# An encoder block on one core: first rows' transposes moved ahead of q's loads, a Fourier copy ahead of a gate's split, more steps between maxima and splits, and steps between first output loads

## Chip, cores and metric

The kernel runs on one core of one Trainium2 chip. The metric is the device time of one execution in microseconds (us), the median of three runs. All work is in one launch; weights, inputs and outputs lie in HBM.

## The reference, cut to what matters

Two batches of 2048 tokens with 1024 channels share one set of weights and go through the same block:

```
u  = rmsnorm(h) ; z = u @ w_in                      # 1024 -> 2304 columns
q, k, v, ga, f, gf = split(z)                       # 512, 128, 128, 512, 512, 512
q, k = rope(rmsnorm(q)), rope(rmsnorm(k))           # per head, 64 wide
a  = softmax(q k^T / 8) v * silu(ga)                # 8 query heads, 2 key/value heads
fo = (real 2-D DFT of f over positions and 64 channels) @ w_fmix * silu(gf)
h  = h + concat(a, fo) @ w_out
h  = h + (p @ w_ple) * sigmoid(rmsnorm(h) @ w_ple_gate)
y  = rmsnorm(h)
```

Everything is float32 in HBM.

## The kernel before

**Products.** A float32 operand is split into two fp16 halves: a power of two scales it, ScalarE (ACT) writes the high half, and VectorE (DVE) writes what is left as the low half (a "split"). Each product is three fp16 matmuls on TensorE (PE). The scale of a weight needs its largest magnitude: eight maxima on DVE, one for each 128 rows, then a maximum over the partitions on GpSimd (`partition_all_reduce`), then a few small DVE operations (`pow2_all`), and then the eight splits.

**Stages.** `project` (the head of the kernel) takes 16 chunks of 256 rows, eight for each batch. For each chunk it forms q, k and v (`mm_tile`), normalises and rotates them, and runs a "sweep" (`sweep_f`, `sweep_ga`) that forms the Fourier input f (two row tiles), the Fourier gate gf (two row tiles, each followed by a small DFT matmul `first` on the f tile) and the attention gate ga (four parts). A sweep is 66 steps; a step of f or gf is three matmuls of 512 columns, a step of ga three of 256. ACT copies f out of PSUM as `ft` at the start of sweep step 9 (first tile) and step 17 (second tile); gf is taken out at steps 25 and 34, ga at 43, 51, 59 and at the first step of what follows. After the head comes the attention, with "fill" work between its steps: first the second half of the DFT (`fourier2`), then the output projection and the rest (`outp`), which goes on when attention is over.

**Order.** In the head the order of each engine's instructions is the order in which Python issues them: every engine is a queue in which an instruction that waits holds all behind it. SyncE (SP) issues most loads, all transposes (DMA) and most stores, in the same order. Background work (`bg`: the other weights' maxima and splits, then the rows of p in `embed_rows`, then `channel_map`) is a generator. `sweep_part(us)` runs sweep steps until their nominal cost is used up, and after every fifth step (`NBF = 5`) takes one piece of `bg`, a piece ending at a `yield`:

```python
us -= next(sweeps[0])
if done:
    done.append(True)
    if len(done) % NBF == 0:
        next(bg, None)
```

`done` is empty for the first `sweep_part` and has one entry from just before the second. `weight_far` has two load pieces, one piece for each of its eight (or two) maxima, one for the scale, and one for each split with its store; it holds two loads ahead. It is called for wo0, pg0, wp0, wo1, pg1, wp1 (`w_out`, `w_ple_gate`, `w_ple` by column half). Tiles of this work and of the sweep share ten slots, `w2k`.

PSUM has eight banks. `bank()` hands them out by a counter: where it is 0 to 4 modulo 8 the tile is `ps_x` (five banks), else `ps_f` (three).

In the start of `project` the order is: first rows of x, weights of k and v, second rows of x, weights of q, and only then the arithmetic on the first rows (`sq_u`, `newton`, `hi_u`, three maxima, `lo_u` with its transpose). In the last four passes (`iteration(16)` to `iteration(19)`) no new rows are formed; the norm and rotation of the last chunks (`lo_q`, `rope_q`, `hi_q`) go on beside the last sweep.

In the fill, `self.after(ticket, n)` yields None until n more attention steps than the ticket's have been flushed; `defer` puts an instruction at the next flush, `defer_slow` at a later one. `outp` starts beside `fourier2` after its tenth tile (`half`) and goes as far as `yield "go"`: a maximum over both branches (`mix_max`, with a `partition_all_reduce`), the loads of the first output tile (`first`, the last entry of which is a GpSimd product), its split, and then go.

Of the kernel before, what the change touches and what calls it, by code (L numbers as in the profile page):

```python
# [139 lines left out]
class Build:  # L140
# [188 lines left out]
    def weight_far(self, name, src, cols, g, pool):  # L329

        nc, st = self.nc, self.st
        sl, ahead, nk = {}, AH, src.shape[0] // 128

        def load(j):
            if j < 2 * nk:
                sl[j] = pool.tile([128, 512], F32, name="w_st", tag="w2k", bufs=self.nw2k)
                nc.sync.dma_start(sl[j][:, :cols], src[j % nk * 128:(j % nk + 1) * 128, :])

        for j in range(ahead):
            load(j)  # L340
            yield
        mx = st.tile([128, 8], F32, name="w_mx")
        for k in range(nk):
            load(k + ahead)
            self.defer(lambda w=sl.pop(k), k=k: nc.vector.tensor_reduce(
                out=mx[:, k:k + 1], in_=w[:, :cols], op=ALU.max, axis=AX.X, apply_absolute_value=True))
            yield
        f = [None] * nk

        def scale():  # L350
            m = mx
            if g is not None:
                m = st.tile([128, 8], F32, name="w_m2")
                nc.vector.tensor_tensor(out=m[:], in0=mx[:], in1=g[:], op=ALU.mult)
            m1 = st.tile([128, 1], F32, name="w_m1")
            nc.vector.tensor_reduce(out=m1[:], in_=m[:, :nk], op=ALU.max, axis=AX.X, apply_absolute_value=True)
            s, self.sc[name] = self.pow2("w_" + name, m1[:], W_EXP)
            f[:] = [s[:]] * nk
            if g is not None:
                gs = st.tile([128, 8], F32, name="w_gs")  # L360
                nc.vector.tensor_scalar(out=gs[:], in0=g[:], scalar1=s[:], scalar2=None, op0=ALU.mult)
                f[:] = [gs[:, k:k + 1] for k in range(nk)]

        self.defer(scale)
        self.wd[name] = nc.dram_tensor("wd_" + name, (128, 2, nk, cols), F16, kind="Internal").ap()
        yield
        for k in range(nk):
            load(k + nk + ahead)
            w = sl.pop(k + nk)
            o = pool.tile([128, 2, 512], F16, name="w_o", tag="w2k", bufs=self.nw2k)  # L370
            nc.scalar.activation(o[:, 0, :cols], w[:, :cols], AF.Copy, scale=f[k])

            def low(k=k, w=w, o=o):
                nc.vector.scalar_tensor_tensor(out=o[:, 1, :cols], in0=w[:, :cols], scalar=f[k], in1=o[:, 0, :cols],
                                               op0=ALU.mult, op1=ALU.subtract)
                nc.sync.dma_start(self.wd[name][:, :, k, :], o[:, :, :cols])

            self.defer(low)
            yield

    def embed_rows(self, pool):

        nc, st = self.nc, self.st
        src = [self.a[n].rearrange("a o (t r) d -> r (a o t) d", t=NT) for n in ("p_prompt", "p_sample")]
        self.ptd = nc.dram_tensor("ptd", (2 * NT, 128, 4, 128), F16, kind="Internal").ap()
        self.pb = self.keep("pb", [128, 2 * NT])
        tl = {}

        def load(i):
            if i < NT:  # L390
                tl[i] = pool.tile([128, 2, 256], F32, name="p_in", tag="w2k", bufs=self.nw2k)
                j = 2 * i % NT
                nc.sync.dma_start(tl[i][:], src[2 * i // NT][:, j:j + 2, :])

        load(0)
        for i in range(NT):
            load(i + 1)
            x, b = tl.pop(i), self.pb[:, 2 * i:2 * i + 2]
            yield
            nc.vector.tensor_reduce(out=b, in_=x[:], op=ALU.max, axis=AX.X, apply_absolute_value=True)  # L400
            nc.vector.tensor_scalar(out=b, in0=b, scalar1=1e-30, scalar2=None, op0=ALU.max)
            nc.vector.tensor_scalar(out=b.bitcast(I32), in0=b.bitcast(I32), scalar1=0x7F800000,
                                    scalar2=None, op0=ALU.bitwise_and)
            f = st.tile([128, 2], F32, name="p_f")
            nc.vector.tensor_scalar(out=f[:].bitcast(I32), in0=b.bitcast(I32), scalar1=-1,
                                    scalar2=(254 + W_EXP) << 23, op0=ALU.mult, op1=ALU.add)
            hl = pool.tile([128, 2, 2, 256], F16, name="p_hl", tag="w2k", bufs=self.nw2k)
            for t in range(2):
                nc.scalar.activation(hl[:, t, 0, :], x[:, t, :], AF.Copy, scale=f[:, t:t + 1])
            yield  # L410
            for t in range(2):
                nc.vector.scalar_tensor_tensor(out=hl[:, t, 1, :], in0=x[:, t, :], scalar=f[:, t:t + 1],
                                               in1=hl[:, t, 0, :], op0=ALU.mult, op1=ALU.subtract)
            pT = pool.tile([128, 2, 4, 128], F16, name="p_T", tag="w2k", bufs=self.nw2k)
            nc.sync.dma_start_transpose(pT[:].rearrange("p t k r -> p (t k) r"), hl[:].rearrange("p t b c -> p (t b c)"))
            yield
            nc.sync.dma_start(self.ptd[2 * i:2 * i + 2].rearrange("t p k r -> p t k r"), pT[:])
            del x, hl, pT
# [125 lines left out]
    def project(self, P, PU, W, early, wkv, wq, wga, bg, mid):  # L544
# [7 lines left out]
        n = len(steps)  # L552
# [177 lines left out]
        def sweep_part(us):  # L730

            while us > 0 and sweeps:
                try:
# [5 lines that stand above are left out]
                        if len(done) % NBF == 2:  # L739
                            next(self.ahead, None)  # L740
                except StopIteration:
                    del sweeps[0]
# [16 lines left out]
        def until(g, word):  # L759
            while next(g) != word:  # L760
                pass

        def iteration(i):
            nonlocal stores, stores_next
            if ok(i + 4):
                load_x(i + 4, 0)
            if ok(i - 1):
                load_rope(i - 1)
            stores, stores_next = stores_next, []
            for f in stores:  # L770
                f()
            del stores[:]
            if ok(i + 3):
                sq_u(i + 3)
            sq = square_z(i - 1) if ok(i - 1) else None
            if ok(i - 1) and i > 2:
                VL.pop((i - 1, 1))()
            if ok(i - 3):
                lo_q(i - 3)
            if ok(i - 2):  # L780
                rope_q(i - 2)
            rs = None
            if ok(i - 1) or ok(i + 2):
                rs = newton(i - 1 if ok(i - 1) else None, i + 2 if ok(i + 2) else None, sq)
            if ok(i):
                mm_tile(i, 0)
            sweep_part(1000.0 if i < n else (5.0, 5.0, 5.0, 100.0)[i - n])
            if ok(i - 1):
                norm_q(i - 1, rs)
            if ok(i + 2):  # L790
                hi_u(i + 2)
                for tt in range(CH):
                    lo_u(i + 2, tt)
            if ok(i + 4):
                load_x(i + 4, 1)
            if ok(i - 2):
                hi_q(i - 2)
            if ok(i):
                VL.pop((i, 0))()
            if ok(i):  # L800
                mm_tile(i, 1)
                append(i)
            if i == n - 3:
                early()
            if i == n + 3:
                self.drain(bg)
                self.drain(self.ahead)
                for f in stores_next:
                    f()
                del stores_next[:]  # L810
# [4 lines left out]
        both(load_x, 0)  # L815
        until(wkv, "loaded")
        both(load_x, 1)
        until(wq, "loaded")
        sq_u(0)
        newton(None, 0, None)  # L820
        hi_u(0)
        for _ in range(3):
            next(wkv)
        both(lo_u, 0)
        until(wkv, "split")
        both(mm_kv, 0)
        until(bg, "loaded")
# [28 lines left out]
        del stores_next[:]  # L856
        append(0)
        until(bg, "split")
        sweep_part(10.0)
        sq_u(2)  # L860
        newton(None, 2, None)
        hi_u(2)
# [3 lines left out]
        until(bg, "split")  # L866
        next(bg)
        done.append(True)
        sweep_part(12.0)
        mid()  # L870
        sq_u(3)
        make_u(3, 0)
# [441 lines left out]
    def outp(self, pool0, ow, open_pool):  # L1314
# [147 lines left out]
        first = load(0)  # L1462
        for f in first[:-1]:
            f()
        yield None
        first[-1]()
        yield from self.after(TM.pop(0))
        yield from self.after(split(0), 2)
        yield "go"
        pool = open_pool()  # L1470
        (wp, gfin), later = self.out_consts(pool)
# [270 lines left out]
```

## Time and profile before

| | before |
|---|---|
| median of three runs | 2787.02 us (2786.7 to 2787.8) |
| the profiled execution | 2787.78 us |
| its span, first to last instruction | 2786.0 us |
| PE busy | 2679.6 us, 96% |
| DVE, POOL, ACT busy | 61%, 59%, 44% |
| granted TensorE clock, mean | 0.987 |

The profiled execution's time is 1.78 us more than its span and 0.76 us more than the median. A row of a timeline has start, duration (both us), engine, line, operation, the tile written and those read, the count of instructions merged into the row, and in brackets how long the engine was idle before it and what ended the wait. SPq and the like are instructions that issue DMAs. A busy share of PE says that a matmul was under way, not how fast it went.

### The profile page before, as it was taken

The page shows a single profiled execution, that of the slowest core. Times are in us where ns is not written, and L with a number is a line of the kernel's source. Part 1 is how long each engine was busy: PE and PEld are TensorE (multiplying, and loading weights), DVE is VectorE, ACT ScalarE, POOL GpSimd, SP SyncE. Part 2 cuts the span into 40 slices and gives each one's busy share as a digit, 9 for nine tenths or more (in the row PEclk, how much of TensorE's full clock was granted, in tenths as well). Part 3 has the DMA queues.
Part 4 walks back from the last instruction along what each step waited for, and adds up shares of the span by engine and source line. Part 5 has one row for each costly group of instructions (what it writes and reads, how often), then busy time and mean ns, then how long its engine had stood idle before and what let it go on. Part 6 is the DMA issues. An engine that isn't in the chain of part 4 may idle for free.

```text
span 2786.0 us, 40443 instructions
## 1 busy us (share of the span) xinstructions
PE 2679.6 (96%) x15332; PEld 1183.4 (42%) x15332; DVE 1691.5 (61%) x2467; ACT 1212.5 (44%) x2047; POOL 1631.6 (59%) x1394
## 2 busy tenths in 40 slices
PE   6799998999998989999999999999999999999998
PEld 3455565565655543333333333333333333333333
DVE  6755546564455765666666666665665665566645
ACT  4433323342224544454544454444444444544442
POOL 1223324242335877777768777767667767677770
PEclk9899999999999999999999999999999999999999
DMA  8467757673427653123221223222322222223223
GB/s 230 142 199 192 200 166 185 174 186 84 139 70 233 216 173 107 46 56 79 64 61 51 61 61 97 78 55 56 74 67 56 61 78 61 54 60 85 56 52 93
DMA packets 418532, 296.37 MB, mean 106 GB/s; under 512 B 259456, under 2 KB 360000, under 8 KB 418336
## 3 DMA queue, kind: packets, MB, share of 16 engines
q1 hardware_dynamic: 405424, 252.01, 34.7%
q0 software_dynamic: 12912, 41.77, 4.5%
q8 instruction: 120, 1.97, 0.3%
q14 instruction: 76, 0.62, 0.1%
HBM read 149.50 MB, written 86.51 MB: 85 GB/s over the span
## 4 chain that ended last, share of the span: by engine, by line
PE 77%; DVE 3%; ACT 1%; issue 1%; POOL 1%; DMA 1%; DVEq 0%; ACTq 0%; POOLq 0%
PE ps_f L429 31%; PE ps_o L1187 15%; PE ps_s L1122 14%; PE ps_x L429 9%; PE ps_m L1149 4%; PE ps_f L1221 1%; PE ps_f L1173 1%; PE ps_f L1041 1%; PE ps_f L995 1%; ACT p L1125 1%; DMA hT<-h_hl 1%; PE ps_x L894 0%; DVE h_hl L1429 0%; DVE a_mx L1157 0%; DVE mh L1352 0%
## 5 line engine op out<-in xcount | busy, mean ns | idle before, releaser
L1130 POOL TENSOR_TENSOR acc<-acc,p 128x1024 f32<-128x1024 f32 x384 | 910.9, 2372 | 245.0 <-ACT p L1125 185.2
L1125 ACT ACTIVATE p<-ps_s,s_scale 128x512 f32<-128x512 f32 x1024 | 648.4, 684 | 748.5 <-PE ps_s L1122 729.3
L1157 DVE TENSOR_REDUCE a_mx<-ps_m 128x1 f32<-128x1024 f32 x499 | 610.3, 1223 | 584.5 <-PE ps_m L1149 583.8
L1187 PE MATMUL ps_o<-p,v 128*64 128x512 f32 x2048 | 465.3, 596 | 0.0
L429 PEld LDWEIGHTS <-uc 128*128 128x128 f16 x3072 | 301.3, 98 | 309.0 <-DMA uc<-hl 23.1
L1122 PE MATMUL ps_s<-q,k 64*128 64x512 f16 x3072 | 425.2, 379 | 6.5 <-ACT p L1125 6.4
L429 PE MATMUL ps_f<-w_pg,hT 128*128 128x512 f16 x1464 | 352.7, 382 | 7.0 <-DMA hT<-h_hl 6.8
L1187 PEld LDWEIGHTS ps_o<-p,v 128*64 128x64 f32 x2048 | 141.6, 137 | 256.5 <-issue 247.5
L1122 PEld LDWEIGHTS <-k 64*128 64x128 f16 x3072 | 115.7, 94 | 307.7 <-issue 236.4
L429 PEld LDWEIGHTS <-hT 128*128 128x128 f16 x1536 | 139.3, 98 | 213.8 <-issue 63.5
L1128 POOL TENSOR_TENSOR acc<-p,p 128x1024 f32<-128x1024 f32 x64 | 150.8, 2357 | 107.8 <-ACT p L1125 107.6
L1149 PE MATMUL ps_m<-k,q 64*128 64x512 f16 x998 | 192.8, 377 | 13.7 <-DVE a_mx L1157 13.7
L429 PE MATMUL ps_f<-w_wo,mh 128*128 128x512 f16 x744 | 181.8, 380 | 4.6 <-DVE mh L1352 4.6
L429 PE MATMUL ps_f<-w_wo,mT 128*128 128x512 f16 x744 | 180.8, 380 | 0.0
L429 PEld LDWEIGHTS <-w_ga 128*128 128x128 f16 x1536 | 153.7, 100 | 37.8 <-issue 17.5
L911 POOL DMA_DIRECT2D gfd<-gt x32 | 19.8, 620 | 228.1 <-DVE gt L939 228.1
L1203 ACT ACTIVATE tb<-ps_o,a_scale 64x256 f32<-64x256 f32 x128 | 60.1, 469 | 162.6 <-PE ps_o L1187 161.8
L929 POOL DMA_DIRECT2D agd<-gat x64 | 35.1, 549 | 147.4 <-DVE gat L939 147.4
L429 PE MATMUL ps_x<-uc,w_ga 128*128 128x256 f16 x1032 | 117.8, 275 | 0.3 <-ACT ge L896 0.3
L1223 DVE RECIPROCAL ps_f<-ps_f 128x256 f32<-128x256 f32 x64 | 112.4, 1756 | 7.2 <-PE ps_f L1221 7.2
L429 PEld LDWEIGHTS <-mh 128*128 128x128 f16 x768 | 68.7, 98 | 108.1 <-issue 33.3
L429 PEld LDWEIGHTS <-mT 128*128 128x128 f16 x768 | 70.0, 98 | 98.9 <-issue 25.4
(283 smaller groups left out, 3330.7 us busy)
## 6 DMA issues: line engine op xcount, KB each, us to landing
q<-qTd SPq DMA_DIRECT2D x256, 64.0 KB, 2.2
ag<-agd SPq DMA_DIRECT2D x64, 256.0 KB, 4.5
out<-h POOLq DMA_DIRECT2D x31, 512.0 KB, 4.0
x<-in_x_prompt SPq DMA_DIRECT2D x16, 512.0 KB, 4.9
w_st<-in_w_out SPq DMA_DIRECT2D x32, 256.0 KB, 4.5
gfd<-gt POOLq DMA_DIRECT2D x32, 256.0 KB, 2.7
gd<-ge POOLq DMA_DIRECT2D x32, 256.0 KB, 3.4
agd<-gat POOLq DMA_DIRECT2D x64, 128.0 KB, 2.7
```

The source lines that it names most:

```text
L429: self.nc.tensor.matmul(ps, lhs(ia, k), rhs(ib, k), start=(i == 0), stop=(i == 3 * ks - 1))
L929: nc.gpsimd.dma_start(self.agd[s][1, r * 128:(r + 1) * 128, c * n:(c + 1) * n], gt[:, :n])
L995: nc.tensor.matmul(o, fT[:, r, y, :], self.bd[:, y, r, :], start=True, stop=x is None)
L1122: nc.tensor.matmul(S[u][e][:], w[sl], q[sl].rearrange("p h q -> p (h q)"), start=j == i == 0, stop=i + 1 == len(todo), skip_group_check=True)
L1125: nc.scalar.activation(p[:, e, :], S[u][e][:], AF.Exp, scale=self.sc["s_scale"][:])
L1128: nc.gpsimd.tensor_tensor(out=ACC[u][:], in0=P[u, 0][:], in1=p[:], op=ALU.add)
L1130: nc.gpsimd.tensor_tensor(out=ACC[u][:], in0=ACC[u][:], in1=p[:], op=ALU.add)
L1149: nc.tensor.matmul(ps[c], Q[u][0][sl, h, :], kt[s, kv, half][sl, :, 0, :], start=True, stop=True)
L1157: nc.vector.reduce_max(MX[u][:, h, half, c:c + 1], x, axis=AX.X)
L1187: nc.tensor.matmul(o[64 * e:64 * e + 64, :], vt[s, kv, c // 8][:, c % 8, :], p[:, e, :], start=(j == 0), stop=(j == 7))
L1203: nc.scalar.activation(tb[64 * e:64 * e + 64], ov[64 - 64 * e:128 - 64 * e, e], AF.Copy, scale=self.sc["a_scale"][64 - 64 * e:128 - 64 * e ...
L1223: nc.vector.reciprocal(r, ps[:, 0:256])
```

## The change

```diff
@@ weight_far
         self.defer(scale)
         self.wd[name] = nc.dram_tensor("wd_" + name, (128, 2, nk, cols), F16, kind="Internal").ap()
-        yield
+        for _ in range(3):
+            yield
         for k in range(nk):
@@ embed_rows
         load(0)
+        yield
+        load(1)
+        yield
         for i in range(NT):
-            load(i + 1)
+            load(i + 2)
             x, b = tl.pop(i), self.pb[:, 2 * i:2 * i + 2]
-            yield
             nc.vector.tensor_reduce(out=b, in_=x[:], op=ALU.max, axis=AX.X, apply_absolute_value=True)
...
             nc.vector.tensor_scalar(out=f[:].bitcast(I32), in0=b.bitcast(I32), scalar1=-1,
                                     scalar2=(254 + W_EXP) << 23, op0=ALU.mult, op1=ALU.add)
+            yield
             hl = pool.tile([128, 2, 2, 256], F16, name="p_hl", tag="w2k", bufs=self.nw2k)
@@ project, iteration
-            sweep_part(1000.0 if i < n else (5.0, 5.0, 5.0, 100.0)[i - n])
+            sweep_part(1000.0 if i < n else (6.0, 9.0, 5.0, 100.0)[i - n])
@@ project, start
         both(load_x, 1)
-        until(wq, "loaded")
         sq_u(0)
         newton(None, 0, None)
         hi_u(0)
         for _ in range(3):
             next(wkv)
         both(lo_u, 0)
+        until(wq, "loaded")
         until(wkv, "split")
@@ project, start
         until(bg, "split")
-        sweep_part(10.0)
+        sweep_part(10.4)
...
         done.append(True)
-        sweep_part(12.0)
+        sweep_part(11.6)
@@ outp
         for f in first[:-1]:
             f()
-        yield None
+        yield from self.after([self.nflush], 3)
         first[-1]()
-        yield from self.after(TM.pop(0))
-        yield from self.after(split(0), 2)
+        yield from self.after(TM.pop(0), 2)
+        yield from self.after(split(0), 1)
         yield "go"
```

`weight_far` has two more empty pieces between the scale and the first split. `embed_rows` loads two tiles ahead instead of one, and the copies that make p's high half go from the maximum's piece into a piece of their own. In the last passes the first two sweep parts get more steps. The two transposes of the first rows are issued ahead of the eight loads of q's weights. The first part of the first sweep goes one step further, and the second as much less. In `outp` some four flushes instead of one fill piece lie between the first loads and the product, two more between product and split, and one less behind the split.

## Rows read from the trace of the kernel before

**Rows 1.** The profile page: span, and busy time of PE and its weight loads, DVE, ACT and GpSimd (POOL) with the share of the span.

```profile
span 2786.0 us, 40443 instructions
...
PE 2679.6 (96%) x15332; PEld 1183.4 (42%) x15332; DVE 1691.5 (61%) x2467; ACT 1212.5 (44%) x2047; POOL 1631.6 (59%) x1394
```

**Rows 2.** The waits of PE in the head (0 to 870 us), the greatest: instruction, what ended the wait, us in total, times, longest.

```profile
PE ps_f L894 <- ACT ft L904: 27.0, 3, 12.5
```

**Rows 3.** Timeline of the start: low halves of the first rows, loads of q's weights, the first rows' transposes, maxima of q's weights, the first matmuls (k and v), the split of q's weights, the matmuls of q.

```profile
10.87 2.48 DVE L627 SCALAR_TENSOR_TENSOR hl<-x,rsq_z,hl 128x1024 f16<-128x1024 f32 x2 [0.24 <-ACT hl L618]
...
11.90 3.52 SPq L292 DMA_DIRECT2D w_t<-in_w_in  x4
...
15.85 7.42 SPq L422 DMA_TRANSPOSE uc<-hl  x2
...
20.50 2.46 DVE L300 TENSOR_REDUCE w_mx<-w_z 128x1 f32<-128x512 f32 x4
...
23.12 8.24 PE L429 MATMUL ps_x<-wr_kv,uc 128*128 128x256 f16 x48 [23.12 <-DMA uc<-hl]
...
31.54 2.73 DVE L323 SCALAR_TENSOR_TENSOR wr_q<-w_z,w_gs,wr_q 128x512 f16<-128x512 f32 x4
32.34 10.41 PE L429 MATMUL ps_x<-wr_q,uc 128*128 128x512 f16 x47 [0.72 <-DVE wr_q L323]
```

**Rows 4.** Timeline of the first sweep: first `ft`, a DFT matmul without a wait, the split of the gate's weight (high halves on ACT, low ones on DVE), and PE behind the second `ft`.

```profile
71.09 0.68 ACT L904 ACTIVATE ft<-ps_x,inv_f 128x512 f32<-128x512 f32 x1
...
73.73 1.02 PE L894 MATMUL ps_x<-ft,dft1x 128*128 128x512 f32 x2
...
86.78 1.33 ACT L322 ACTIVATE w_ga<-w_qn,w_gs 128x512 f16<-128x512 f32 x2 [8.00 <-DVE w_gs L316]
...
88.86 4.05 DVE L323 SCALAR_TENSOR_TENSOR w_ga<-w_t,w_gs,w_ga 128x512 f16<-128x512 f32 x6
...
92.41 2.08 PE L894 MATMUL ps_f<-ft,dft 128*128 128x512 f32 x2 [12.48 <-ACT ft L904]
...
94.28 4.22 PE L429 MATMUL ps_f<-uc,w_ga 128*128 128x256 f16 x24
```

**Rows 5.** Busy time of each engine in two stretches behind a stall; the eighth column is the granted clock of PE.

```profile
92.40:97.20 4.80, 4.79 (x16) 2.76 (x17) 4.66 (x19) 4.23 (x8) 2.35 (x4) 0.50 0.47 158
97.20:105.00 7.80, 7.80 (x74) 6.95 (x73) 7.14 (x39) 1.56 (x4) 1.08 (x2) 1.00 0.20 76
```

**Rows 6.** Timeline of the second sweep, where wo0 gets its scale: last DVE step of the maximum, the maximum over partitions, first splits, `ft`, PE, and the copy `ge` that frees the bank for which the gate's second part waits.

```profile
135.48 0.15 DVE L356 TENSOR_REDUCE w_m<-w_mx 128x1 f32<-128x8 f32 x1
138.90 0.38 POOL L254 PARTITION_ALL_REDUCE p_mm<-w_m  x1 [5.92 <-issue]
...
139.87 1.33 ACT L371 ACTIVATE w_o<-w_st,w_wo_s 128x512 f16<-128x512 f32 x2 [13.84 <-DVE w_wo_s L265]
...
141.83 2.08 PE L894 MATMUL ps_x<-ft,dft 128*128 128x512 f32 x2 [6.10 <-ACT ft L904]
...
146.79 0.59 ACT L896 ACTIVATE ge<-ps_x 128x512 f32<-128x512 f32 x1
...
147.43 2.78 PE L429 MATMUL ps_x<-uc,w_ga 128*128 128x256 f16 x24 [0.31 <-ACT ge L896]
```

**Rows 7.** Timeline of the fifth sweep, where wo1 gets its scale.

```profile
296.15 0.38 POOL L254 PARTITION_ALL_REDUCE p_mm<-w_m  x1 [6.00 <-issue]
...
299.68 5.28 PE L429 MATMUL ps_f<-uc,w_ga 128*128 128x256 f16 x24 [3.92 <-DVE gat L939]
```

**Rows 8.** Timeline of the eighth sweep, where the rows of p begin: the first maximum, PE, and a copy that waits for a slot.

```profile
447.90 0.69 DVE L400 TENSOR_REDUCE pb<-p_in 128x2 f32<-128x512 f32 x1 [3.92 <-DMA p_in<-in_p_prompt]
...
450.76 2.08 PE L894 MATMUL ps_f<-ft,dft 128*128 128x512 f32 x2 [8.68 <-ACT ft L904]
...
452.63 4.24 PE L429 MATMUL ps_f<-uc,w_ga 128*128 128x256 f16 x24
...
457.05 0.60 ACT L896 ACTIVATE ge<-ps_f 128x512 f32<-128x512 f32 x1 [2.27 <-DMA ptd<-p_T]
```

**Rows 9.** Timeline of the end of the head: the last chunk's `hi_q`, PE behind its stall, the first attention matmul, and the first load of the Fourier fill.

```profile
845.58 1.06 ACT L703 ACTIVATE qs<-t 128x1024 f16<-128x1024 f32 x1 [12.99 <-POOL t L691]
...
847.88 2.08 PE L894 MATMUL ps_f<-ft,dft 128*128 128x512 f32 x2 [5.79 <-ACT ft L904]
...
862.29 0.39 PE L1122 MATMUL ps_s<-mr,kone 64*128 64x512 f16 x2 [1.02 <-DVE gat L939]
...
865.71 0.80 SPq L969 DMA_DIRECT2D g_in<-gd  x2
```

**Rows 10.** The same load by its tile (first of the two), from issue to landing, and the first Fourier matmul on PE.

```profile
DMA to landing us min/median/max: 4.2/4.2/4.2
...
870.38 2.82 PE L1041 MATMUL ps_f<-c,g_in 128*128 128x128 f32 x16
```

**Rows 11.** Timeline of the attention about the maximum over both branches: GpSimd's first product behind it, PE, the first output tile's split on ACT, PE.

```profile
990.66 2.33 POOL L1130 TENSOR_TENSOR acc<-acc,p 128x1024 f32<-128x1024 f32 x1 [9.81 <-issue]
...
998.56 0.61 PE L1149 MATMUL ps_m<-k,q 64*128 64x512 f16 x2 [9.80 <-DVE a_mx L1157]
...
1003.86 1.15 ACT L1347 ACTIVATE mh<-ag,mix_s 128x1024 f16<-128x1024 f32 x1 [15.96 <-POOL ag L1333]
...
1006.12 0.37 PE L1122 MATMUL ps_s<-q,k 64*128 64x512 f16 x1 [1.65 <-ACT p L1125]
```

## The prediction

> **What bounds the kernel now.** I read the page, then the waits of PE, then the timeline about each long wait. PE is busy in 96% of the span, the others in 61% or less [rows 1], so what counts is where PE stands still, and how fast it runs behind that. PE's list of waits has six long stalls, and each edit lies beside one. Three, 27.0 us together, wait for `ft` [rows 2]: ACT had to make the copy behind a split whose scale was late. They are 12.48 us in the first sweep [rows 4], 8.68 us at the rows of p [rows 8] and 5.79 us at the end of the head [rows 9]. A fourth `ft`, at wo0, costs 6.10 us [rows 6]; at wo1 PE stands 3.92 us for a bank [rows 7]; at the maximum over both branches 9.80 us [rows 11]. Together 46.8 us.
>
> A stall costs more than its length. Behind the 12.48 us PE had a granted clock of 0.50 (the 1.2 GHz level) for about 5 us, then 1.00 [rows 5]: the two DFT matmuls took 2.08 us instead of 1.02 and 24 gate matmuls 4.22 us [rows 4] instead of 2.78 [rows 6], so 2.5 us more. The stall of 3.92 us costs the same: 5.28 for 2.78 [rows 7].
>
> The question is what comes next in each stage once ACT is out of the way. In the middle of the head PE feeds itself, and a removed stall stays removed; at the start and at the end a chain over the other engines sets the time.
>
> **The transposes ahead of q's loads: +2.5 us.** The low halves of the first rows are done at 13.4 (10.87 + 2.48); the transposes were issued at 15.85 behind q's loads, and k's and v's matmuls began at 23.12. They could now begin at about 18, when their weights' split is under way (an estimate from these rows). But q's matmuls, next on PE, don't wait for that: they began at 32.34 with the low half of q's weights, at the end of a DVE chain that is busy nearly throughout (maxima 20.50, split 31.54) [rows 3]. So k and v end near 26 instead of 31.4, and PE stands still for 5 to 6 us ahead of q. After 3.92 us it lost 2.5 us; I take +2.5. The eight loads are issued from about 17 on; at 0.88 us each [rows 3] and the 4.2 us to landing of a load of that size [rows 10] the first four are there by about 24, where their maxima end at 23.0. A wait there can reach the 7.42 us that the two transposes held SP [rows 3], less some 5 us of lead, so 2.5 us. Bounds: 0 (the clock stays up) to +5. This delay runs on through q and the first sweep, since DVE's maxima for gf and so the gate's split stand behind them. f's eight loads, next on SP, are wanted only after q's split, which covers them.
>
> **The Fourier copy, and wo0's pieces: -2.4 us.** 10.0 was used up after 16 steps of 0.64, 10.4 after 17, and the 17th begins with the copy; 11.6 ends where 12.0 did. So `ft` stands ahead of `sq_u(2)` and costs ACT 0.67 us, by which all behind it, the gate's split too, is late. PE then goes through its DFT matmul at 80 and stops at the gate itself, whose first product needs the split: low halves end at 92.91, now 93.6. That product ended at 98.50 (94.28 + 4.22) [rows 4], so PE has 4.9 us.
>
> They don't last. Two empty pieces move wo0's first split from step 9 of the second sweep to step 20 (bg pieces come after steps 5m + 16 now, 5m + 15 before), so `ft` passes it, and the 6.10 us go. But the scale is asked for at step 5, and DVE's small operations stand right behind it: DVE is done with the maximum at 135.48, GpSimd yields it at 138.90 after 5.92 us in which it waits for nothing shown, and the first split runs at 139.87 [rows 6]. Gate part two needs the bank that `ge` frees, and `ge` stands behind that split. So: 139.87 + 0.67 late + 0.67 split + 0.67 + 0.59 for the two copies = 142.5, where it began at 147.43 [rows 6]. That is 4.9 us for both edits, less 2.5 us for a PE that has again stood about 6 us: -2.4. Bounds: 0, and -12.1 (4.9, 6.10 and 1.06 of slow DFT matmuls) if the chain is no limit.
>
> The 5.92 and 6.00 us recur at each such maximum [rows 6, 7]. The Trainium skill (GPSIMD Engine Reference, Instruction dispatch) says that the first call of a freshly loaded GpSimd kernel pays about 6 us of loading, with no instruction to show for it; the rows agree. Taken alone it says that pieces between scale and split take none of it away, and the sum would be the second rival's.
>
> **wo1: -6.4 us.** The pieces added earlier (2 each at wo0, pg0, wp0, wo1) shift its scale from step 31 of the fifth sweep to step 62. At 31 DVE stood still with gf's second tile and all the gate's still to take out, and three `ps_f` banks were full; at 62 three gate parts are out. 3.92 + 2.5 [rows 7]. Counting banks for the other scales (steps 44, 53, 35, 44 of sweeps 3, 4, 7, 8) I find none where PE would run out within 6 us. Bounds: -6.4 to 0 (another place stalls instead).
>
> **Rows of p: -10.0 us.** The copies stand at step 18 now, behind `ft` at 17, and the loads two tiles ahead, so DVE's 3.92 us for the load go too. 8.68 + 1.06 + 1.46 (4.24 for 2.78) = 11.2 [rows 8]. I give 1.2 back: in this sweep the gate's third part needs a bank that a late DVE frees. Bounds: -11.2 to -6.
>
> **Last passes: 0.** Ten and fifteen steps instead of eight and eight put both `ft` and the first gate copy ahead of the last `hi_q`, and PE is spared 5.79 us and 1.06 of slow DFT matmuls. But the first Fourier matmul, four attention steps on, needs a load that SP issues at 865.71 and that lands 4.2 us later, 869.9 [rows 9, 10]; PE was there at 870.38. SP is held by the last chunk's transposes and stores, these by `hi_q` at 845.58, and that by GpSimd [rows 9]; no edit touches this chain. So PE comes about 7 us early and waits. Bounds: -6.9, and +2.5 (it is slow after the wait).
>
> **`outp`: -1.7 us.** The 9.80 us are DVE's wait for GpSimd, which came back at 990.66, 9.81 us after its maximum; no edit touches that. ACT stood 15.96 us before the split because the product was late, and PE lost 1.65 to that [rows 11]; with six flushes more it doesn't. Bounds: -1.7 to 0; the later go is hidden by the end of `fourier2`.
>
> **Sum.** +2.5 - 2.4 - 6.4 - 10.0 + 0 - 1.7 = -18.0; 2787.8 - 18.0 = 2769.8 for the profiled execution, 0.76 less for the median: 2769.0.
>
> **Rivals.**
> *All stalls go.* If no chain limits, 0 - 12.1 - 6.4 - 11.2 - 6.9 - 1.7 = -38.3, and 2787.0 - 38.3 = 2748.7. For it: each stall's releaser is passed. Against: 139.87 and 869.9 hang on other engines.
> *GpSimd's 6 us move along.* DVE still stands through each, so wo0 and wo1 give nothing: +2.5 - 10.0 - 1.7 = -9.2: 2777.8. Against: of the six such maxima of far weights only wo0's and wo1's stand beside a stall of PE.
> *Slots run out (slower).* Far weights hold two loaded tiles ten steps longer, and the rows of p three tiles instead of two, of ten slots. ACT already waited 2.27 us for one [rows 8]. If each of the sixteen turns adds that on PE's path: 36.3 us, and 2787.0 + 18.3 = 2805. It decides from eight turns on. Against: PE stood for none of them before.
> *No change that can be told* (within 0.2%, 5.6 us, about what a measurement of this kernel can tell): the other engines' chains take all back. Against: at wo1 and at the rows of p, 16.4 us of the sum, the rows show no such chain.
>
> **How the numbers follow.** Forecast 0.60, all go 0.13, GpSimd's move along 0.13, slots 0.07, no change 0.07. Faster 0.86, same 0.07, slower 0.07. Three quarters of the way from the forecast to the first rival is 2754; the second rival and half of the way from it to no change 2782. What lies outside is the slots, no change, and the far part of the first rival, about 0.2.
>
> **What would show it.** Right: matmuls of k and v begin near 18 and q's run slow; no `ft` in PE's waits; PE stands about 7 us at the gate's split and 6 us ahead of gate part two in the second sweep; nothing at wo1; a new wait of about 6 us, of the first Fourier matmul for its load; 9.8 us as before at the maximum, without ACT's 15.96. Wrong: q's maxima wait for loads; ACT or DVE waits for slots reach PE; the end of the head comes 7 us sooner.

## The result and the profile after

The changed kernel took 2769.88 us (median of six runs, 2765.7 to 2777.6), the kernel before 2786.08 us in the same comparison (2782.5 to 2787.8). The ratio is 0.9947, 95% interval 0.9932 to 0.9962: faster. The forecast was 2769.0 us within 2754 to 2782. The total is right; two terms of the sum are not. In the second of the two profiles below their errors cancel, which is luck; in the first only one of them shows. Two executions, one with the transposes undone (2803.55 us, the profiled one) and one with the stores moved (3101.08 us), ran at a mean granted clock of 0.967 and 0.848 where all others had 0.985 or more; they stand outside the medians, and the first one's trace is not used.

The profiled execution took 2765.67 us and is the fastest of its six. So a second profile of the same kernel (the first experiment, 2770.24 us) stands beside it below.

The page of the changed kernel, span and busy time, answers to [rows 1]. PE's busy time fell by 4.7 us and the span by 22.1: what went is standing still.

```profile
span 2763.9 us, 40442 instructions
...
PE 2674.9 (97%) x15332; PEld 1181.3 (43%) x15332; DVE 1684.7 (61%) x2467; ACT 1211.4 (44%) x2047; POOL 1630.8 (59%) x1394
```

PE's waits of the changed kernel up to 1060 us (what ended the wait, us in total, times, longest). Of the waits for `ft` [rows 2] 0.6 us is left. Other names are long instead: the split of q's weights, the split of the gate's, the copy `ge` (0.31 us before [rows 6]), and `g_in`.

```profile
PE ps_m L1153 <- DVE a_mx L1161: 13.7, 5, 9.6
PE ps_f L433 <- ACT w_ga L322: 7.3, 1, 7.3
PE ps_x L433 <- ACT wr_q L322: 7.3, 1, 7.3
PE ps_f L1045 <- DMA g_in<-gd: 5.2, 1, 5.2
PE ps_s L1126 <- ACT p L1129: 4.5, 11, 0.8
PE ps_x L433 <- ACT ge L900: 3.1, 1, 3.1
```

The best view of such a change is the start of the same matmul in both traces. Below, for each place, its start minus the start in the kernel before (negative is earlier); the places are named by their time before. The first line is the sum on record.

```
place (us before)       42.6  106.2  155.3  307.7  464.6    800    873   1200    end
prediction, cumulated   +2.5           0.1   -6.3  -16.3  -16.3  -16.3  -18.0  -18.0
changed kernel         +2.85  -1.81  -4.40 -11.27 -22.58 -20.58 -21.14 -19.89  -22.1
the same, 2nd profile  +3.91  -0.75  -4.63  -6.36 -17.68 -15.25 -16.14 -15.24  -17.6
```

From 307.7 on the second profile lies within 1.4 us of the forecast up to 873. The first is about 5 us earlier from 307.7 on, and that arises at one place, wo1. The rows of the timeline that answer to [rows 3, 6, 9]: start, second sweep, end of the head, each of the changed kernel.

```profile
12.19 5.16 SPq L426 DMA_TRANSPOSE uc<-hl  x2
...
17.40 8.23 PE L433 MATMUL ps_x<-wr_kv,uc 128*128 128x256 f16 x48 [17.40 <-DMA uc<-hl]
...
21.31 2.09 DVE L300 TENSOR_REDUCE w_mx<-w_z 128x1 f32<-128x512 f32 x3 [0.73 <-DMA w_z<-in_w_in]
...
32.94 0.58 PE L433 MATMUL ps_x<-wr_q,uc 128*128 128x512 f16 x1 [7.31 <-ACT wr_q L322]
...
34.03 11.57 PE L433 MATMUL ps_x<-wr_q,uc 128*128 128x512 f16 x47 [0.51 <-DVE wr_q L323]
...
138.56 0.38 POOL L254 PARTITION_ALL_REDUCE p_mm<-w_m  x1 [5.95 <-issue]
...
141.36 4.28 PE L433 MATMUL ps_x<-uc,w_ga 128*128 128x256 f16 x24 [3.13 <-ACT ge L900]
...
833.76 0.39 PE L1126 MATMUL ps_s<-mr,kone 64*128 64x512 f16 x2 [1.08 <-DVE gat L943]
...
843.96 0.80 SPq L973 DMA_DIRECT2D g_in<-gd  x2
...
848.35 3.75 PE L1045 MATMUL ps_f<-c,g_in 128*128 128x128 f32 x16 [5.16 <-DMA g_in<-gd]
```

### The profile page after: what moved, and what is told of

The parts are those of the page before. It is cut to its first block, busy times and chain, and to the rows that moved or that the text cites. A ratio compares the mean times of both kernels' runs of the same rounds, so it can differ in the third digit from the quotient of the medians.

```text
span 2763.9 us, 40442 instructions
## 1 busy us (share of the span) xinstructions
PE 2674.9 (97%) x15332; PEld 1181.3 (43%) x15332; DVE 1684.7 (61%) x2467; ACT 1211.4 (44%) x2047; POOL 1630.8 (59%) x1394
## 4 chain that ended last, share of the span: by engine, by line
PE 78%; DVE 3%; issue 3%; DMA 2%; POOL 1%; ACT 1%; SPq 0%; DVEq 0%; POOLq 0%; ACTq 0%
PE ps_f L433 31%; PE ps_o L1191 15%; PE ps_s L1126 14%; PE ps_x L433 9%; PE ps_m L1153 4%; PE ps_f L1225 1%; PE ps_f L1177 1%; PE ps_f L1045 1%; PE ps_f L999 1%; ACT p L1129 1%; DMA hT<-h_hl 0%; DMA w_st<-in_w_out 0%; DVE a_mx L1161 0%; DMA g_in<-gd 0%; DMA w_st<-in_w_ple_gate 0%
```

## The experiments

Each undoes or adds one thing in the changed kernel, but for two near the end that combine. The ratio is against the kernel before in the same group of runs; the changed kernel's was 0.9947 and 0.9943.

**The changed kernel again.** No edit.

> The changed kernel as it is, beside the undone versions of this group. Its six runs lay between 2765.7 and 2777.6 us, twice the spread of the kernel before. Expected: a median within 2 us of 2769.9. If the spread is of the kernel, some waits differ from one execution to the next, and the profile shows where; if it was chance, the runs lie within 5 us.

Measured: 2770.24 us (2769.6 to 2778.7), ratio 0.9943 (0.9929 to 0.9956). The wide spread is no mark of the change: over 23 runs the kernel before spread as far (2780.8 to 2792.7). But the two profiled executions do differ at one place, wo1, where PE stands in this one, as before [rows 7], and doesn't in the first. Second profile, DVE's first maximum of wo1, its first gate product, and PE:

```profile
286.06 0.69 DVE L345 TENSOR_REDUCE w_mx<-w_st 128x1 f32<-128x512 f32 x1 [4.70 <-DMA w_st<-in_w_out]
...
293.97 0.42 DVE L943 SCALAR_TENSOR_TENSOR gat<-th,ps_f 128x256 f32<-128x256 f32 x1 [3.61 <-DMA gd<-ge]
...
294.44 4.44 PE L433 MATMUL ps_f<-uc,w_ga 128*128 128x256 f16 x24 [3.32 <-DVE gat L943]
```

And the same two on DVE, with PE, in the first profile. DVE is 3 us earlier, early enough for PE, whose row runs through:

```profile
282.88 0.69 DVE L345 TENSOR_REDUCE w_mx<-w_st 128x1 f32<-128x512 f32 x1 [4.68 <-DMA w_st<-in_w_out]
...
290.52 0.42 DVE L943 SCALAR_TENSOR_TENSOR gat<-th,ps_f 128x256 f32<-128x256 f32 x1 [2.62 <-DMA gd<-ge]
...
285.95 8.02 PE L433 MATMUL ps_f<-uc,w_ga 128*128 128x256 f16 x72
```

The wait is not the scale's (that comes at 302.75 and 307.36 now): DVE, which works in order, waits for wo1's first load, and the gate's copies behind it come late. 3.32 us of standing and 1.66 us of slow clock (4.44 for 2.78, with a granted clock of 0.51 from 294.4 to 297.7) are the 5 us.

DVE waits as long for the load in both, 4.70 and 4.68 us, so the 3 us are older. They are there at wo0's fourth split on ACT, in the first profile and in the second:

```profile
146.91 0.72 ACT L372 ACTIVATE w_o<-w_st,w_wo_s 128x512 f16<-128x512 f32 x1 [2.17 <-DMA gd<-ge]
```

```profile
150.28 0.72 ACT L372 ACTIVATE w_o<-w_st,w_wo_s 128x512 f16<-128x512 f32 x1 [4.16 <-DMA gd<-ge]
```

Of these 3.37 us about 1.4 are older still (the first split ran at 139.53 and 140.96), and 1.99 are a longer wait for a slot that a store holds. The background work keeps such a lag. In eight profiles without a piece more at wo1, wo1's first maximum follows the last of wo0's splits by 127.1 to 128.8 us, though these lie between 153.4 and 158.1; in that of the sweep parts at 10.0 it follows by 130.0.

**The transposes behind q's loads again.**

```
+        until(wq, "loaded")
         sq_u(0)
...
         both(lo_u, 0)
-        until(wq, "loaded")
```

> The transposes of the first rows behind q's loads again, all else changed. Theory (absorbed): the 2.85 us that k's and v's second matmuls come later never reach the end, because in the second sweep gate part two waits for the Fourier copy behind wo0's split, whose maximum hangs on SP's loads; PE waits there about 6 us instead of 3.13, and the end moves by -0.5 to +0.5 us. Rival (carried, as the prediction had it): the delay runs on through the head, and the end comes 2.85 us sooner. Either way k's and v's first matmuls begin near 23 instead of 17.4.

Measured: 2766.24 us, ratio 0.9918 (0.9910 to 0.9927), an interval that doesn't touch that of the changed kernel. The rival was right: the move costs, 4.0 us between the medians. I had read "absorbed" from the start of wo0's maximum, which hardly differs before and after; the reason is another one (below, at the second term). Two later kernels with the same undo show the start. In the last one (the output's start, below) q's matmuls run at full clock, 10.41 us, and PE stands 0.72 us:

```profile
23.75 7.60 PE L433 MATMUL ps_x<-wr_kv,uc 128*128 128x256 f16 x48 [23.75 <-DMA uc<-hl]
...
32.57 10.41 PE L433 MATMUL ps_x<-wr_q,uc 128*128 128x512 f16 x47 [0.72 <-DVE wr_q L323]
```

**One empty piece between maximum and split.**

```
-        for _ in range(3):
-            yield
+        yield
```

> One empty piece instead of three between the maximum and the first split of the far weights, all else changed. Theory: gate part two of the second sweep begins near 147 instead of 141.4, which costs 4.4 us up to q's next matmuls, and the stall at wo1 is back, 6.4 to 6.9 us: +9.5 to +11.3 in all, less 1 to 2 us that drift back later. Rival (GpSimd's 6 us move along, whatever stands between): 0. Second rival (wo1 alone): +6.9.

Measured: 2788.95 us, ratio 1.0005 (0.9995 to 1.0015): +18.7, the whole gain, and more than the theory's 11.3. "GpSimd's 6 us move along" falls. PE's long waits of the second and fifth sweep are back, longer than before [rows 6, 7], since PE comes earlier and the scales later; a third, of 3.73 us and for a bank, stands behind the eighth:

```profile
144.34 2.08 PE L897 MATMUL ps_x<-ft,dft 128*128 128x512 f32 x2 [8.59 <-ACT ft L907]
...
304.92 4.29 PE L432 MATMUL ps_f<-uc,w_ga 128*128 128x256 f16 x24 [7.07 <-DVE gat L942]
...
466.84 2.78 PE L432 MATMUL ps_x<-wr_kv,uc 128*128 128x256 f16 x24 [3.73 <-DVE gat L942]
```

By starts it lies 6.7 us behind the second profile at 155.3, 10.3 at 307.7, 10.9 at 464.6, 13.9 at 478, 17.4 at the end, so some 6 us arise outside the two places of the theory. The edit also brings forward all background work behind wo0's scale, the rows of p by twelve pieces; what the pieces do at the scales and what they do as a shift can't be told apart here.

**The last passes at five steps.**

```
-            sweep_part(... (6.0, 9.0, 5.0, 100.0)[i - n])
+            sweep_part(... (5.0, 5.0, 5.0, 100.0)[i - n])
```

> The last passes at five steps each again, all else changed. Theory: the load of the first Fourier matmul sets when PE goes on; PE stands about 6 us for the Fourier copy and no more for the load, and the end moves by 0 to +1 us. Rival (the passes themselves are worth what PE is spared): +7 us.

Measured: 2771.46 us, ratio 0.9935 (0.9922 to 0.9948): no difference. The `ft` stall is back and the load's wait falls from 5.16 to 0.84 us; between 800 and 873 this kernel gains 0.3 us on the kernel before, the changed one 0.6 and 0.9.

```profile
832.45 2.07 PE L898 MATMUL ps_f<-ft,dft 128*128 128x512 f32 x2 [5.80 <-ACT ft L908]
...
855.62 2.02 PE L1045 MATMUL ps_f<-c,g_in 128*128 128x128 f32 x16 [0.84 <-DMA g_in<-gd]
```

**The rows of p as before.**

```
         load(0)
-        yield
-        load(1)
-        yield
         for i in range(NT):
-            load(i + 2)
+            load(i + 1)
...
+            yield
             nc.vector.tensor_reduce(...)
...
-            yield
             hl = pool.tile(...)
```

> The rows of p as before (copies in the piece behind the scale's, loads one tile ahead), all else changed. Theory: PE stands at the first copy again, 8 to 9 us, and runs slow behind it: +10 to +11.3 us, as the aligned starts of the two kernels gave 11.3. Rival (the other pieces have moved the rows of p past the place where it hurts): 0 to +3.

Measured: 2780.32 us, ratio 0.9971 (0.9960 to 0.9983): +10.1 to +10.4 between the medians, +7 to +8 by the ratios. The size is about the predicted one, but not at one place: PE no longer stands 8.68 us [rows 8], but 1.91, 2.88 and 1.68 us at 449, 478 and 643, and 5.2 us are lost between 464.6 and 560. The copies meet the sweeps elsewhere, 12 pieces later.

**The sweep parts at 10.0 and 12.0.**

> The first two sweep parts at 10.0 and 12.0 again, so that the first Fourier copy stands behind the squares and the gate's split, all else changed. Locally PE loses about 6 us in the first sweep (12.5 us of standing for 7.3, and 1.06 us of slow matmuls). Theory (absorbed): 3.13 us of standing and 1.5 us of slow clock in the second sweep go in exchange, and the end moves by +1 to +3. Rival (carried): +6.

Measured: 2769.77 us, ratio 0.9932 (0.9919 to 0.9946): nothing lost. PE stands 12.49 us for `ft` again (95.43), and at 155.3 the kernel is 3.9 us behind the second profile; at 307.7 it is at -6.59, against -6.36, since PE stands only 0.84 us at wo1. Against that profile, what the copy wins is gone again at wo1, where PE goes on when DVE lets it; against the first one, which doesn't stand there, the kernel stays 4.7 us behind. That the copy is worth nothing rests on the medians, not on one profile.

**Five pieces for wo0.**

```
-        for _ in range(3):
+        for _ in range({"wo0": 5, "pg0": 1}.get(name, 3)):
```

> Five empty pieces for wo0 and one for pg0 instead of three each, so that all later pieces stay where they are. The Fourier copy that frees the bank of gate part two then stands ahead of wo0's first split. Theory: the 3.13 us of standing at gate part two and 1.5 us of slow clock go: -4.6 us. Rival: DVE, which still waits for GpSimd until 139, holds the banks or the copies instead, and PE waits for it: 0 to -1.

Measured: 2772.06 us, ratio 0.9946 (0.9933 to 0.9958): nothing. The wait for `ge` is gone and q's next matmuls start at 147.32 instead of 150.65; at wo1 PE then stands 6.53 us instead of 3.32. The theory was right at its place, its sum wrong.

```profile
294.32 5.17 PE L433 MATMUL ps_f<-uc,w_ga 128*128 128x256 f16 x24 [6.53 <-DVE gat L943]
```

**The last stores on GpSimd's queue.**

```
+            dq = nc.gpsimd if i == n - 1 else nc.sync
...
-            nc.sync.dma_start(self.qTd[s][t], qT[:])   (and kTd)
+            dq.dma_start(self.qTd[s][t], qT[:])
```

> The last chunk's stores of q and k go out on GpSimd's queue at the end of the head instead of on SP's, which frees SP about 4.5 us earlier. Theory (SP's chain sets the first Fourier matmul): its load is issued near 839.5 instead of 843.96 and lands near 843.5, PE no longer waits 1.24 us for q nor 5.16 us for the load: -3 to -6 us. Rival: GpSimd stands for the transposes instead, its sums come late and PE waits for their slots: 0 or slower.

The edit also issues them later, behind the head's last background work. Measured: 2768.65 us, ratio 0.9931 (0.9917 to 0.9944): no difference that can be told. PE no longer waits for q. From the first score matmul to the first Fourier matmul it takes 12.73 us (838.69 to 851.42) instead of 14.59, so 1.9 us came of the 4.4 that SP was freed (its q loads start 1.62 us behind the first score matmul, 6.00 us in the changed kernel): the four now take 3.98 us to issue instead of 2.40, and the load 5.13 us to land instead of 4.25. The load is still what PE waits for:

```profile
840.31 3.98 SPq L1114 DMA_DIRECT2D q<-qTd  x4
...
846.25 0.80 SPq L975 DMA_DIRECT2D g_in<-gd  x2
...
851.42 1.86 PE L1047 MATMUL ps_f<-c,g_in 128*128 128x128 f32 x7 [5.42 <-DMA g_in<-gd]
```

**One more piece ahead of wo1's maximum.**

```
+        if name == "wo1":
+            yield
         mx = st.tile([128, 8], F32, name="w_mx")
...
-        for _ in range(3):
+        for _ in range(2 if name == "pg1" else 3):
```

> The changed kernel with one more empty piece between wo1's first loads and its first maximum, and one less at pg1, so that the pieces behind keep their places. In most executions of the changed kernel PE stood about 3 us near 291 for the gate, since DVE had waited 4.7 us for wo1's first load and the tanh and the product behind it then waited for a slot held by a store. Theory (the load comes late for its maximum): DVE no longer waits there, PE doesn't stand and runs at full clock: -4 to -5 us, and a spread like that of the kernel before. Rival (slots: ten are too few whatever the order): DVE's wait goes, the wait for a slot stays, 0 to -1.

Measured: 2768.35 us (2762.4 to 2770.5), ratio 0.9931 (0.9919 to 0.9944). In the profile PE runs through wo1 without a wait (-10.56 at 307.7), though DVE still waits 4.43 us for the load. The medians differ by 1.5 to 1.9 us, within the intervals: not shown. Nor did PE stand about 3 us there "in most executions", as I expected: of the nine profiles with the changed kernel's order at wo1, three have more than 1 us (3.32, 2.03 with the last passes at five steps, 6.53 with five pieces).

**Nine slots.** `self.nw2k = 9`.

> The changed kernel with nine slots of 2 KB instead of ten, nothing else. Theory (the other engines' chain in the second to eighth sweeps is held by slots that stores set free about 4 us after they are issued): waits of ACT and DVE for slots grow, PE stands at wo1 in every execution and at other far weights too: +5 to +20 us. Rival (slots are no limit, the loads and GpSimd are): 0 to +2.

Measured: 2769.79 us, ratio 0.9942 (0.9929 to 0.9956). The rival was right: slots are no limit, and "Slots run out" falls with it, although single rows name a slot's holder (`gd<-ge` above).

**Three together.** The undone transposes, wo1's piece, the stores.

> The changed kernel with three things together: the transposes of the first rows behind q's loads again, one more piece ahead of wo1's first maximum (one less at pg1), and the last chunk's stores of q and k on GpSimd's queue. Theory: -4 us for the first as it was measured, -4 to -5 for the second, -2 for the third; the first two may be the same gain: -5 to -10 against the changed kernel, near 2762. Rival (each only takes the place of another wait): 2766 as with the first alone.

Measured: 2766.01 us, ratio 0.9925 (0.9912 to 0.9938): the rival. At 155.3 it lies at -8.37, 4.0 and 3.7 us ahead of the two profiles of the changed kernel, at 800 at -24.29, 3.7 us ahead of the first profile; between 1006 and 1200 it loses 5.3 us again. Its PE there:

```profile
1012.00:1018.00 6.00, 3.60 (x28) 1.99 (x27) 5.93 (x9) 3.05 (x6) 6.00 (x5) 0.98 0.57 178
1018.00:1024.00 6.00, 5.60 (x14) 1.57 (x15) 2.76 (x4) 0.35 (x1) 5.47 (x4) 0.50 0.51 169
```

The first number behind the length is PE's busy time, the eighth column its granted clock. PE waits 1.18 and 1.41 us for DVE, which is busy for 5.93 of the first 6 us, and then runs at 0.50.

**The output's start as before**, with the transposes undone.

```
-        yield from self.after([self.nflush], 3)
+        yield None
         first[-1]()
-        yield from self.after(TM.pop(0), 2)
-        yield from self.after(split(0), 1)
+        yield from self.after(TM.pop(0))
+        yield from self.after(split(0), 2)
```

> The changed kernel with the transposes of the first rows behind q's loads again and the steps between the first output loads as before. In the changed kernel and seven of its versions PE was 0.8 to 4.5 us later against the kernel before at 1200 than at 873, behind waits of up to 1.2 and 1.4 us for DVE's maxima near 1020. Theory (those waits come from the edit of the output's start): between 873 and 1200 nothing is lost to the kernel before, PE's 1.65 us and ACT's 15.96 us are back, and the time is 1 to 4 us below that with the transposes alone undone: 2762 to 2765. Rival (the edit spares PE 1.7 us, as predicted, and the later waits come from elsewhere): 2767 to 2768.

Measured: 2766.99 us, ratio 0.9925 (0.9913 to 0.9938): the rival's time, and of its two reasons the second. ACT stands its 15.9 us again, and PE lost 0.42 us to it, not the 1.65 of the kernel before [rows 11]. Near 1020 PE waits 0.49 and 0.57 us at a granted clock of 1.00, and so it does in the second profile, which has the edit (the clock is 0.72 from 1028 to 1034 there). From 873 to 1200 this kernel loses 1.0 us to the kernel before; the two profiles of the changed one 1.3 and 0.9, three versions with the edit 4.1 to 4.5.

## Why the prediction was right and where it wasn't

**Transposes, predicted +2.5.** The sign, the size and the course held: k and v from 17.40 (about 18), 7.31 us of standing (5 to 6), +2.85 and +3.91 at 42.6. Its parts differ. q's maxima waited for their loads, 0.73 us in the row above, which the prediction had named as a sign of being wrong; and q began 1.69 us late (32.94 for 31.25, the first of its matmuls in both traces). Only 1.16 us was slow clock (11.57 for 10.41 [rows 3]; the granted clock was 0.50 from 32.9 to 36.3). The row of before:

```profile
31.25 0.38 PE L429 MATMUL ps_x<-wr_q,uc 128*128 128x512 f16 x1
```

The delay does run on to the end, 4.0 us in the medians. Single traces don't carry it so evenly: of the two kernels with the undone move, the three together keep 3.7 to 4.0 us of it at 155.3, the last only 0.8 to 1.1.

**Copy and wo0, predicted -2.4, measured -7.25 (-4.40 less 2.85), and -8.5 in the second profile.** This is the step that failed. "The chain is no limit" was rightly turned down: PE stood 3.13 us for `ge`, not about 6, and ran slow behind it, 1.5 us instead of 2.5 (in the second profile it stood 3.59 us and then ran at full clock, 2.78 us). But gate part two began at 141.36, not at 142.5 plus the 2.5 of the first term. The delays never reached wo0's maximum (135.12, where it ran at 135.48 before), since DVE's low halves of the third rows, ahead of it, became shorter. Before, then after:

```profile
104.63 0.77 POOL L567 TENSOR_TENSOR rt<-rt,g_k_t 128x256 f32<-128x256 f32 x1
105.65 2.33 POOL L669 TENSOR_TENSOR qn<-z,q_rs 128x1280 f32<-128x1280 f32 x1 [0.24 <-DVE q_rs L610]
...
106.03 6.32 DVE L627 SCALAR_TENSOR_TENSOR hl<-x,rsq_z,hl 128x1024 f16<-128x1024 f32 x2 [0.46 <-ACT hl L618]
```

```profile
108.28 2.96 DVE L631 SCALAR_TENSOR_TENSOR hl<-x,rsq_z,hl 128x1024 f16<-128x1024 f32 x2 [0.81 <-ACT hl L622]
...
108.49 1.66 POOL L571 TENSOR_TENSOR rt<-rt,g_k_t 128x256 f32<-128x256 f32 x1
110.12 3.31 POOL L673 TENSOR_TENSOR qn<-z,q_rs 128x1280 f32<-128x1280 f32 x1
```

3.36 us shorter, beside GpSimd, which is itself slower now. With 1.0 less of slow clock that is 4.4 of the 4.5 us missing by 155.3 (0.1 forecast, -4.40 measured). With the sweep parts as before, GpSimd's 128x1280 product starts first again and the low halves take 5.97 us:

```profile
108.70 2.33 POOL L673 TENSOR_TENSOR qn<-z,q_rs 128x1280 f32<-128x1280 f32 x1 [0.52 <-DVE q_rs L614]
...
109.44 5.97 DVE L631 SCALAR_TENSOR_TENSOR hl<-x,rsq_z,hl 128x1024 f16<-128x1024 f32 x2 [0.81 <-ACT hl L622]
```

So the prediction priced the order on ACT, and not what the new order does to DVE and GpSimd, which run beside each other there.

**wo1, predicted -6.4: -6.87 in one profile, -1.73 in the other.** From 155.3 to 307.7 six of the nine profiles with this order gain 5.9 to 6.9 us, so the term is the usual case. (Six pieces lie ahead of this scale, those of three weights; the prediction lists a fourth, but its 31 steps fit the six.) The scale went where it was said to go, and its wait with it. What I left out is the new neighbour: wo1's first maxima now stand where the scale stood, wait 4.0 to 4.7 us for the first load in all traces with that order, and DVE's work for the gate queues up behind them. This fits the bound "another place stalls instead". It can also take back what PE has won earlier, as the profile with five pieces shows. Whether PE is caught depends on how late DVE is in that execution, and that is settled at wo0's splits, 128 us earlier; why the store that holds the slot there is 2 us slower in one execution is open.

**Rows of p, predicted -10.0.** -11.31 and -11.32 up to 464.6; by 800 2.0 and 2.4 are given back, where 1.2 were reckoned. Undone it costs 7 to 10 us.

**Last passes, predicted 0.** -0.6 and -0.9, with the wait of about 6 us where it was said to be: 5.16, and 1.24 for q. The 4.25 us from issue to landing agree with the 4.2 [rows 10].

**Output's start, predicted -1.7.** It is worth nothing that can be told: without the edit PE loses 0.42 us there in the changed kernel, not the 1.65 of the row of before, and in some executions later waits cost 3 us more. One profile without the edit is too little to say whether these waits come from it.

**The sum.** In the second profile the errors are -4.7 by 155.3 and +4.7 at wo1; the forecast then holds by cancelling, which is luck. In the first the second one is missing, and the end is at -22.1. For the median, near the second profile's time, only the total is known.

**A faster version.** The change without the moved transposes took 2766.24 us, 0.9918 of the kernel before. The other additions gave nothing on top that the runs can tell.

## What to carry to other kernels

A stall that is taken away on PE pays only as far as the next place where another engine's chain sets the time, so cumulate the differences of the same instruction's start over both traces, and look at such places, before adding terms up. An absolute time read from a chain ("the split runs at 139.87") must be shifted by the delays that the same change puts ahead of that chain, and by what the new order does to engines that run side by side. Pieces that only postpone work can be the whole gain, and one profile can be the lucky execution.

## What the runs showed of the hardware

DVE's low halves of two 128x1024 tiles took 2.96 us where they started ahead of GpSimd's second 128x256 product (108.28 against 108.49), and 6.32 us where GpSimd's 128x1280 product was already under way (105.65 against 106.03). In turn the 128x256 product took 1.66 instead of 0.77 us and the 128x1280 one 3.31 instead of 2.33. Between the two, four versions in which only the 128x256 product had begun first, by 0.05 to 0.46 us, took 4.62 to 5.03 us. The Trainium skill says that the two share a pair of ports under an exclusive lock, and that the order of issue decides who blocks (SBUF — State Buffer, Who interferes with whom); these durations agree with that in kind. So a shift of 0.26 us between the two engines (DVE 0.21 us ahead of the 128x256 product in the changed kernel, 0.05 behind it with one empty piece) goes with 2.1 us on DVE's chain, and the order of before with 3.4.

The maxima over partitions still have some 6 us ahead of them in which GpSimd waits for nothing shown: 5.95 us at wo0 in the changed kernel, 6.07 with one piece, 5.92 before [rows 6]. More pieces don't shorten it; PE just has other work meanwhile.
